# A fused LoRA kernel on one core: stores issued from ScalarE, loads from SyncE, matmuls that lower semaphores

## Chip, core and metric

One core of one Trainium2 chip. The metric is the device time of one execution in microseconds; lower is better. A core has five engines that run their own instruction streams (TensorE or PE, VectorE or DVE, ScalarE or ACT, GpSimd or POOL, SyncE or SP) and meet at semaphores, and 16 DMA engines that move data between HBM and the on-chip memory.

## The reference

```
x: (16, 512, 768) float32   A: (768, 16)   B: (16, 768)   scale = 0.5
lora = np.matmul(np.matmul(x, A), B)
return (x + scale * lora).astype(np.float32)
```

Every element of x is read once and every element of the result is written once: 25.2 MB in and 25.2 MB out, with two thin matrix products between them.

## The kernel before

**Tokens.** The 8192 tokens are 64 tiles of 128. They are held in six parts of 2, 6, 8, 16, 16 and 16 tiles (PARTS). In a part of S tiles a partition holds S tokens that lie next to each other in memory, so one partition's row in a transfer is S x 3072 bytes. The on-chip memory has three rooms of 16 tiles; ROOM says where a part lies. The last part is put where the first three parts were, so its two loads wait until these are stored.

**Transfers.** LOADS and STORES list seven transfers each, as (part, first tile, number): parts 0 to 4 whole, and part 5 in two halves. In this document L0 to L6 and S0 to S6 are these in order. All fourteen are issued by SP: L0 to L4 at once, then S0, S1 and S2, each when VectorE's sums for it are done (s_sum), then L5 when S0 and S1 have landed (s_out0), L6 when S2 has (s_out1), then S3 to S6. ScalarE issues the loads of A and B. They go into every eighth partition of a_rows and b_rows, which are cleared first by VectorE (L209) and GpSimd (L164).

**Work on a group.** Eight tiles are a group, and there are eight groups (0 to 7). L0 and L1 hold group 0, L2 group 1, L3 groups 2 and 3, L4 groups 4 and 5, L5 group 6, L6 group 7. For each group:
- narrowed() makes a float16 copy xh of x, four tiles on ScalarE (q = 0) and four on GpSimd (q = 1), all at L158;
- turned() transposes xh in 32 x 32 blocks on VectorE (L233, two instructions);
- projected() multiplies by A on TensorE (L261, 24 matmuls in three thirds);
- spread() scales that product and puts it on the diagonal blocks of y_bd, on ScalarE (L197, four instructions);
- raised() multiplies a pair of tiles by B on TensorE (L275, four matmuls) into one of two buffers lora;
- VectorE adds lora to x in place (L243, one instruction for a pair).

**Order.** Each engine's order is written out by hand. TensorE runs the four raised() of one group between the thirds of projected() of the next. Its first pass raises a group that doesn't exist, from a y_bd of zeros, to fill the loop. VectorE runs turned(g + 1) and then the four adds of g. ScalarE runs spread(g) and then narrowed(g + 2). Behind the last add of a group that ends a store VectorE drains and raises s_sum (L247). TensorE takes a semaphore in two steps, a wait and a separate sem_inc of -1 (take()); one semaphore s_free counts the lora buffers that VectorE has emptied.

**Start.** A is transposed (L211) and copied into w_one and w_bd (L218, L226) on VectorE; B is narrowed to b_half (L189), multiplied by a picking matrix (L285) and copied to b_mm (L191) on ScalarE.

Of the kernel before, what the change touches and what calls it, by code (L numbers as in the profile page):

```python
# [22 lines left out]
APART = 8  # L23
# [3 lines left out]
def kernel(  # L27
# [11 lines left out]
    Q = 32  # L39
# [39 lines left out]
    def sem(name):  # L79
        sems.append(nc.alloc_semaphore(name))  # L80
        return sems[-1]
# [9 lines left out]
    def memory(t2, i, s, n):  # L91
        S = PARTS[i]
        return t2[ds(parts[i], S * P), :].rearrange("(p s) d -> p s d", s=S)[:, ds(s, n), :]

    def held(i, s, n):
        r, s0 = ROOM[i]
        return rooms[r][:, ds(s0 + s, n), :]
# [8 lines left out]

    s_a, s_b = sem("s_a"), sem("s_b")
    s_brows, s_pick, s_bh, s_bp = sem("s_brows"), sem("s_pick"), sem("s_bh"), sem("s_bp")
    s_ready, s_zero, s_w, s_bm = sem("s_ready"), sem("s_zero"), sem("s_w"), sem("s_bm")
    s_nact, s_npool = sem("s_nact"), sem("s_npool")  # L110
    s_turned, s_y, s_spread = sem("s_turned"), sem("s_y"), sem("s_spread")
    s_lora, s_free, s_sum = sem("s_lora"), sem("s_free"), sem("s_sum")
    s_out0, s_out1, s_out = sem("s_out0"), sem("s_out1"), sem("s_out")

    MMS = 2 * NC
# [5 lines left out]
    def groups_for(i, s, n):  # L121
        return where.index((i, s + n - 1)) // GROUP + 1
# [8 lines left out]
    @block.sync  # L131
    def _(e):
        def load(ld):
            e.dma_start(out=held(*ld), in_=memory(x2, *ld)).then_inc(s_load[ld], 16)

        def store(st, done):
            e.wait_ge(s_sum, STORED.index(groups_for(*st)) + 1)
            e.dma_start(out=memory(out2, *st), in_=held(*st)).then_inc(done, 16)

        load(LOADS[0])  # L140
        for ld in LOADS[1:5]:
            load(ld)
        for st, done in zip(STORES, (s_out0, s_out0, s_out1)):
            store(st, done)
        e.wait_ge(s_out0, 32)
        load(LOADS[5])
        e.wait_ge(s_out1, 16)
        load(LOADS[6])
        for st in STORES[3:]:
            store(st, s_out)  # L150

    def narrowed(e, copy, done, g, q):
        t = g * GROUP + q * SUB
        for s in dict.fromkeys(load_sem(t + k) for k in range(SUB)):
            e.wait_ge(s, 16)
        if g >= 2:
            e.wait_ge(s_y, g - 1)
        copy(  # L158
            out=xh[g % 2][:, ds(q * SUB, SUB), :], in_=held(*where[t], SUB)
        ).then_inc(done, 1)  # L160

    @block.gpsimd
    def _(e):
        e.memset(b_rows, 0.0).then_inc(s_brows, 1)  # L164
        e.memset(pick, 0.0).then_inc(s_pick, 1)
        e.memset(w_bd.rearrange("p c k m -> p (c k m)").bitcast(fp32), 0.0)  # L166
        for t in y_bd:
            e.memset(t.rearrange("p s m -> p (s m)").bitcast(fp32), 0.0)  # L168
        e.wait_ge(s_pick, 1)
        e.affine_select(  # L170
            out=pick, in_=pick, compare_op=mybir.AluOpType.not_equal, fill=1.0, base=0,
            pattern=[[0, NQ], [-APART, Q]], channel_multiplier=1,
        ).then_inc(s_zero, 1)
        for g in range(NG):
            narrowed(e, e.tensor_copy, s_npool, g, 1)

    @block.scalar
    def _(e):
        e.wait_ge(s_brows, 1)
        e.dma_start(  # L180
            out=b_rows[0 : R * APART : APART, :], in_=B
        ).then_inc(s_b, 16)
        e.wait_ge(s_ready, 1)
        e.dma_start(
            out=a_rows[0 : NC * APART : APART, :],
            in_=A.rearrange("(c e) r -> c (e r)", e=64),
        ).then_inc(s_a, 16)
        e.wait_ge(s_b, 16)
        e.copy(out=b_half, in_=b_rows).then_inc(s_bh, 1)  # L189
        e.wait_ge(s_bp, 1)  # L190
        e.copy(out=b_mm, in_=lora[0][:, 0, :]).then_inc(s_bm, 1)  # L191

        def spread(g):
            e.wait_ge(s_y, g + 1)
            for b in range(NQ):
                q = ds(b * Q, Q)
                last = e.mul(out=y_bd[g % 2][q, :, q], in_=y_ps[g % 2][q, :, :], mul=sc)  # L197
            last.then_inc(s_spread, 1)

        narrowed(e, e.copy, s_nact, 0, 0)  # L200
        narrowed(e, e.copy, s_nact, 1, 0)
        for g in range(NG):
            spread(g)
            if g + 2 < NG:
                narrowed(e, e.copy, s_nact, g + 2, 0)

    @block.vector
    def _(e):
        e.memset(a_rows, 0.0).then_inc(s_ready, 1)  # L209
        e.wait_ge(s_a, 16)  # L210
        e.transpose(  # L211
            out=a_t[0 : NC * APART].rearrange("i k r c -> i (k r) c"),
            in_=a_rows[0 : NC * APART].rearrange("c (i k r) -> c (k r) i", k=2, r=R),
        ).then_inc(s_ready, 1)
        e.wait_ge(s_ready, 2)
        EACH = Q // APART
        for b in range(NC // EACH):
            last = e.tensor_copy(  # L218
                out=w_one[:, ds(b * EACH, EACH), :, :],
                in_=a_t[ds(b * Q, Q)].rearrange("i k r (c n) -> i c k r n", n=APART)[..., 0],  # L220
            )
        last.then_inc(s_ready, 1)
        e.wait_ge(s_ready, 3)
        e.wait_ge(s_zero, 1)
        for b in range(NQ):
            last = e.tensor_copy(out=w_bd[ds(b * Q, Q), :, :, ds(b * Q, R)], in_=w_one)  # L226
        last.then_inc(s_w, 1)

        def turned(g):
            for q, s in ((0, s_nact), (1, s_npool)):  # L230
                e.wait_ge(s, g + 1)
                v = xh[g % 2][:, ds(q * SUB, SUB), :].bitcast(fp32)
                last = e.transpose(out=v, in_=v)  # L233
            last.then_inc(s_turned, 1)

        turned(0)
        for g in range(NG):
            if g + 1 < NG:
                turned(g + 1)
            for p in range(PAIRS):  # L240
                xs = held(*where[g * GROUP + 2 * p], 2)
                e.wait_ge(s_lora, (g + 1) * PAIRS + p + 1)
                e.tensor_tensor(  # L243
                    out=xs, in0=xs, in1=lora[p % 2], op=mybir.AluOpType.add
                ).then_inc(s_free, 1)
            if g + 1 in STORED:
                e.drain().then_inc(s_sum, 1)  # L247

    @block.tensor
    def _(e):  # L250
        def take(s):
            e.wait_ge(s, 1)
            e.sem_inc(s, -1)  # L253

        def projected(h, steps):
            if steps[0] == 0:
                take(s_turned)
            xv = xh[h].rearrange("p s (c j k) -> p s c j k", c=NC, k=2)
            for m in steps:
                c, k = divmod(m, 2)  # L260
                last = e.matmul(  # L261
                    y_ps[h], w_bd[:, c, k, :], xv[:, :, c, :, k],
                    start=(m == 0), stop=(m == MMS - 1),
                )
            if steps[-1] == MMS - 1:
                last.then_inc(s_y, 1)

        def raised(h, p):
            if p == 0:
                take(s_spread)  # L270
            take(s_free)
            t = lora[p % 2]
            for k in range(2):
                for n0, w in ((0, 512), (512, 256)) if k == 0 else ((0, 256), (256, 512)):
                    last = e.matmul(  # L275
                        t[:, k, ds(n0, w)], y_bd[h][:, 2 * p + k, :], b_mm[:, ds(n0, w)],
                        start=True, stop=True,
                    )
            last.then_inc(s_lora, 1)


        e.wait_ge(s_bh, 1)
        e.wait_ge(s_zero, 1)
        for n0, w in ((0, 512), (512, 256)):
            last = e.matmul(  # L285
                lora[0][:, 0, ds(n0, w)], pick.rearrange("p b r -> p (b r)"),
                b_half[:, ds(n0, w)], start=True, stop=True,
            )
        last.then_inc(s_bp, 1)
        e.sem_inc(s_spread, 1)  # L290
        e.sem_inc(s_free, 2 + PAIRS)
        e.wait_ge(s_w, 1)
        e.wait_ge(s_bm, 1)
        with e.Fori(0, NG // 2):
            for h in range(2):
                raised(1 - h, 0)
                raised(1 - h, 1)
                projected(h, range(0, THIRD))
                raised(1 - h, 2)
                projected(h, range(THIRD, 2 * THIRD))  # L300
                raised(1 - h, 3)
                projected(h, range(2 * THIRD, MMS))
        for p in range(PAIRS):
            raised(1, p)
# [43 lines left out]
```

## Time and profile before

| | us |
|---|---|
| median of 3 runs | 124.85 (124.49 to 125.08) |
| profiled execution, its own time | 124.84 |
| its span in the profile | 122.9 |
| VectorE busy | 87.0 (71%) |
| TensorE matmuls busy | 53.9 (44%) |
| ScalarE busy | 36.9 (30%) |
| GpSimd busy | 25.6 (21%) |
| DMA, mean over the span | 410 GB/s |

Span and busy times are of one execution, and so are the lines of the profile in this document; the difference of 1.94 us between the span and the execution's own time lies outside the span. A page cuts the span into 40 slices, with a digit for the busy share in tenths. A group line ends in its busy time, the mean of one instruction, the idle time before the group's instructions and what ended it. In the timeline a line is start, duration, engine, line and operation, with the idle time before it in brackets. In the waits a line is who waited for whom, the total in us, how often, and the longest. A DMA packet in the trace's records is one partition's row, or the 4 bytes that raise a semaphore at the end.

### The profile page before, as it was taken

The page shows a single profiled execution, that of the slowest core. Times are in us where ns is not written, and L with a number is a line of the kernel's source. Part 1 is how long each engine was busy: PE and PEld are TensorE (multiplying, and loading weights), DVE is VectorE, ACT ScalarE, POOL GpSimd, SP SyncE. Part 2 cuts the span into 40 slices and gives each one's busy share as a digit, 9 for nine tenths or more (in the row PEclk, how much of TensorE's full clock was granted, in tenths as well). Part 3 has the DMA queues.
Part 4 walks back from the last instruction along what each step waited for, and adds up shares of the span by engine and source line. Part 5 has one row for each costly group of instructions (what it writes and reads, how often), then busy time and mean ns, then how long its engine had stood idle before and what let it go on. Part 6 is the DMA issues. An engine that isn't in the chain of part 4 may idle for free. (4 is left out here: it accounts for less than half of the span.)

```text
span 122.9 us, 967 instructions
## 1 busy us (share of the span) xinstructions
PE 53.9 (44%) x338; PEld 31.8 (26%) x338; DVE 87.0 (71%) x57; ACT 36.9 (30%) x43; POOL 25.6 (21%) x18
## 2 busy tenths in 40 slices
PE   0002068768306994493483477449438353000000
PEld 0000034445103562262242254236225221000000
DVE  2006993959729989999999999999999789300000
ACT  0416608220199106708504082640400400000000
POOL 7402608000196001708000080440000000000000
PEclk9999999999995599999999999999999999555555
DMA  3999999799799795999999999999899799799990
GB/s 98 429 415 450 416 528 432 336 512 480 304 496 496 320 464 228 490 418 432 456 392 464 432 400 480 400 496 448 352 480 496 336 464 466 325 456 400 456 440 40
DMA packets 2074, 50.46 MB, mean 410 GB/s; under 512 B 252, under 2 KB 252, under 8 KB 536
## 3 DMA queue, kind: packets, MB, share of 16 engines
q1 hardware_dynamic: 2016, 50.33, 96.5%
q10 hardware_dynamic: 56, 0.10, 0.2%
q8 instruction: 1, 0.02, 0.0%
q14 instruction: 1, 0.01, 0.0%
HBM read 25.26 MB, written 25.17 MB: 410 GB/s over the span
## 5 line engine op out<-in xcount | busy, mean ns | idle before, releaser
L243 DVE TENSOR_TENSOR x_sb<-x_sb,lora_ps 128x1536 f32<-128x1536 f32 x32 | 53.8, 1740 | 3.5 <-PE lora_ps L275 3.5
L275 PE MATMUL lora_ps<-b_mm,y_bd 128*128 128x512 f16 (+1 forms) x144 | 30.9, 351 | 30.8 <-PEq L253 30.8
L158 POOL CAST xh<-x_sb 128x3072 f16<-128x3072 f32 x8 | 21.9, 2746 | 55.0 <-DMA x_sb<-in_x_dram 50.5
L233 DVE STREAM_TRANSPOSE xh<-xh 128x1536 f32<-128x1536 f32 x16 | 27.5, 1755 | 5.4 <-ACT xh L158 5.0
L261 PE MATMUL ps_yt<-xh,w_bd 128*128 128x256 f16 x192 | 26.1, 277 | 9.0 <-PEq L253 9.0
L158 ACT CAST xh<-x_sb 128x3072 f16<-128x3072 f32 x8 | 22.0, 2752 | 18.2 <-DMA x_sb<-in_x_dram 18.2
L275 PEld LDWEIGHTS lora_ps<-b_mm,y_bd 128*128 128x128 f16 x144 | 13.2, 102 | 44.6 <-issue 38.9
L261 PEld LDWEIGHTS ps_yt<-xh,w_bd 128*128 128x128 f16 x192 | 18.4, 98 | 16.9 <-issue 12.0
L197 ACT ACTIVATE y_bd<-ps_yt 32x256 f16<-32x256 f32 x32 | 12.0, 374 | 34.3 <-PE ps_yt L261 34.0
L211 DVE STREAM_TRANSPOSE a_t<-a_rows 96x1024 f32<-96x1024 f32 x1 | 1.9, 1926 | 8.3 <-DMA a_rows<-in_A_dram 8.3
L285 PE MATMUL lora_ps<-b_half,pick 128*128 128x512 f16 (+1 forms) x2 | 0.8, 514 | 9.6 <-ACT b_half L189 9.6
L285 PEld LDWEIGHTS lora_ps<-b_half,pick 128*128 128x128 f16 x2 | 0.1, 110 | 9.6 <-ACT b_half L189 9.6
L218 DVE CAST w_one<-a_t 32x128 f16<-32x128 f32 x3 | 2.5, 836 | 0.1
L189 ACT ACT_TABLE_LOAD x1 | 1.3, 1283 | 3.7 <-issue 3.7
L189 ACT CAST b_half<-b_rows 128x768 f16<-128x768 f32 x1 | 0.8, 832 | 3.7 <-DMA b_rows<-in_B_dram 3.7
L209 DVE MEMSET a_rows<- 128x1024 f32 x1 | 0.9, 912 | 1.2 <-SPq L127 1.2
L166 POOL MEMSET w_bd<- 128x1536 f32 x1 | 1.4, 1382 | 0.0
L191 ACT CAST b_mm<-lora_ps 128x768 f16<-128x768 f32 x1 | 0.8, 798 | 0.9 <-PE lora_ps L285 0.9
L226 DVE COPY w_bd<-w_one 32x384 f16<-32x384 f16 x4 | 1.0, 251 | 0.1
L168 POOL MEMSET y_bd<- 128x512 f32 x2 | 1.0, 524 | 0.0
L164 POOL MEMSET b_rows<- 128x768 f32 x1 | 0.7, 737 | 0.5 <-SPq L127 0.5
L170 POOL TENSOR_SCALAR_AFFINE_SELECT pick<-pick 128x128 f16<-128x128 f16 x1 | 0.3, 309 | 0.0
(5 smaller groups left out, 0.6 us busy)
## 6 DMA issues: line engine op xcount, KB each, us to landing
x_sb<-in_x_dram SPq DMA_DIRECT2D x2, 6144.0 KB, 38.1
out_dram<-x_sb SPq DMA_DIRECT2D x2, 6144.0 KB, 22.9
x_sb<-in_x_dram SPq DMA_DIRECT2D x3, 3072.0 KB, 15.1
out_dram<-x_sb SPq DMA_DIRECT2D x3, 3072.0 KB, 16.4
x_sb<-in_x_dram SPq DMA_DIRECT2D x1, 2304.0 KB, 10.1
out_dram<-x_sb SPq DMA_DIRECT2D x1, 2304.0 KB, 22.3
x_sb<-in_x_dram SPq DMA_DIRECT2D x1, 768.0 KB, 4.5
out_dram<-x_sb SPq DMA_DIRECT2D x1, 768.0 KB, 17.2
```

The costliest lines, as they stand in the source:

```text
L158: copy(out=xh[g % 2][:, ds(q * SUB, SUB), :], in_=held(*where[t], SUB)).then_inc(done, 1)
L166: e.memset(w_bd.rearrange("p c k m -> p (c k m)").bitcast(fp32), 0.0)
L168: e.memset(t.rearrange("p s m -> p (s m)").bitcast(fp32), 0.0)
L189: e.copy(out=b_half, in_=b_rows).then_inc(s_bh, 1)
L197: last = e.mul(out=y_bd[g % 2][q, :, q], in_=y_ps[g % 2][q, :, :], mul=sc)
L211: e.transpose(out=a_t[0 : NC * APART].rearrange("i k r c -> i (k r) c"), in_=a_rows[0 : NC * APART].rearrange("c (i k r) -> c (k r) i", k= ...
L218: last = e.tensor_copy(out=w_one[:, ds(b * EACH, EACH), :, :], in_=a_t[ds(b * Q, Q)].rearrange("i k r (c n) -> i c k r n", n=APART)[..., 0],)
L226: last = e.tensor_copy(out=w_bd[ds(b * Q, Q), :, :, ds(b * Q, R)], in_=w_one)
L233: last = e.transpose(out=v, in_=v)
L243: e.tensor_tensor(out=xs, in0=xs, in1=lora[p % 2], op=mybir.AluOpType.add).then_inc(s_free, 1)
L261: last = e.matmul(y_ps[h], w_bd[:, c, k, :], xv[:, :, c, :, k], start=(m == 0), stop=(m == MMS - 1),)
L275: last = e.matmul(t[:, k, ds(n0, w)], y_bd[h][:, 2 * p + k, :], b_mm[:, ds(n0, w)], start=True, stop=True,)
```

## The change

Five things are changed together.
- Stores are issued by ScalarE: stored(g) stands behind spread(g) and narrowed(g + 2) and issues those stores whose last group is g - 1. SP issues only loads.
- A and B are issued by SP behind L1 and before L2. Both areas are cleared by GpSimd, a_rows first.
- TensorE's matmuls lower the semaphores themselves (then_inc with -1); s_free becomes four semaphores, one for each pair of a group. GpSimd sets the first values that TensorE set, and VectorE waits for the four raised() of the first pass before turned(1).
- On ScalarE narrowed(0) comes before the copy of b_mm, and narrowed() there no longer waits for s_y.
- The last s_sum is raised by the last add itself, without a drain.

```diff
-        def store(st, done):
-            e.wait_ge(s_sum, STORED.index(groups_for(*st)) + 1)
-            e.dma_start(out=memory(out2, *st), in_=held(*st)).then_inc(done, 16)
-
         load(LOADS[0])
-        for ld in LOADS[1:5]:
+        load(LOADS[1])
+        e.wait_ge(s_ready, 1)
+        e.dma_start(
+            out=a_rows[0 : NC * APART : APART, :], in_=A.rearrange("(c e) r -> c (e r)", e=64)
+        ).then_inc(s_a, 16)
+        e.wait_ge(s_brows, 1)
+        e.dma_start(out=b_rows[0 : R * APART : APART, :], in_=B).then_inc(s_b, 16)
+        for ld in LOADS[2:5]:
             load(ld)
-        for st, done in zip(STORES, (s_out0, s_out0, s_out1)):
-            store(st, done)
         e.wait_ge(s_out0, 32)
         load(LOADS[5])
         e.wait_ge(s_out1, 16)
         load(LOADS[6])
-        for st in STORES[3:]:
-            store(st, s_out)
...
-        if g >= 2:
+        if q and g >= 2:
             e.wait_ge(s_y, g - 1)
...
+        e.memset(a_rows[0 : NC * APART], 0.0).then_inc(s_ready, 1)
         e.memset(b_rows, 0.0).then_inc(s_brows, 1)
+
+        e.sem_inc(s_spread, 1)
+        for s in s_free[2:]:
+            e.sem_inc(s, 1)
...
+        def stored(groups):
+            for st in STORES:
+                if groups_for(*st) == groups:
+                    done = s_out0 if groups == 1 else s_out1 if groups == 2 else s_out
+                    e.wait_ge(s_sum, STORED.index(groups) + 1)
+                    e.dma_start(out=memory(out2, *st), in_=held(*st)).then_inc(done, 16)
+
         for g in range(NG):
             spread(g)
             if g + 2 < NG:
                 narrowed(e, e.copy, s_nact, g + 2, 0)
 
+            stored(g)
+        stored(NG)
...
         turned(0)
+        for p in range(PAIRS):
+            e.wait_ge(s_lora, p + 1)
+            e.sem_inc(s_free[p], 1)
...
-                ).then_inc(s_free, 1)
-            if g + 1 in STORED:
+                )
+                if g + 1 < NG or p + 2 < PAIRS:
+                    ins.then_inc(s_free[p], 1)
+                elif p + 1 == PAIRS:
+                    ins.then_inc(s_sum, 1)
+            if g + 1 in STORED[:-1]:
                 e.drain().then_inc(s_sum, 1)
...
-            if steps[-1] == MMS - 1:
+            if steps[0] == 0:
+                last.then_inc(s_turned, -1)
+            elif steps[-1] == MMS - 1:
                 last.then_inc(s_y, 1)
...
-                take(s_spread)
-            take(s_free)
+                e.wait_ge(s_spread, 1)
+            free = s_free[(p + 2) % PAIRS]
+            e.wait_ge(free, 1)
...
+            if p == 0:
+                mms[0].then_inc(s_spread, -1)
+            mms[1].then_inc(free, -1)
+            mms[-1].then_inc(s_lora, 1)
```

More of the change, by code (lines that the diff above doesn't have):

```diff
@@ L108 @@
     s_brows, s_pick, s_bh, s_bp = sem("s_brows"), sem("s_pick"), sem("s_bh"), sem("s_bp")
-    s_ready, s_zero, s_w, s_bm = sem("s_ready"), sem("s_zero"), sem("s_w"), sem("s_bm")
+    s_ready, s_zero, s_bm = sem("s_ready"), sem("s_zero"), sem("s_bm")
     s_nact, s_npool = sem("s_nact"), sem("s_npool")
     s_turned, s_y, s_spread = sem("s_turned"), sem("s_y"), sem("s_spread")
-    s_lora, s_free, s_sum = sem("s_lora"), sem("s_free"), sem("s_sum")
+    s_lora, s_sum = sem("s_lora"), sem("s_sum")
+    s_free = [sem(f"s_free{p}") for p in range(PAIRS)]
     s_out0, s_out1, s_out = sem("s_out0"), sem("s_out1"), sem("s_out")
@@ L178, in _ @@
     def _(e):
[L179 to L187, printed above, removed]
+        e.wait_ge(s_zero, 1)
         e.wait_ge(s_b, 16)
         e.copy(out=b_half, in_=b_rows).then_inc(s_bh, 1)
-        e.wait_ge(s_bp, 1)
-        e.copy(out=b_mm, in_=lora[0][:, 0, :]).then_inc(s_bm, 1)
         def spread(g):
@@ L200, in _ @@
         narrowed(e, e.copy, s_nact, 0, 0)
+        e.wait_ge(s_bp, 1)
+        e.copy(out=b_mm, in_=lora[0][:, 0, :]).then_inc(s_bm, 1)
         narrowed(e, e.copy, s_nact, 1, 0)
+        def stored(groups):
[4 more added lines that the diff above has]
+                    e.dma_start(out=memory(out2, *st), in_=held(*st)).then_inc(done, 16)
         for g in range(NG):
@@ L205, in _ @@
                 narrowed(e, e.copy, s_nact, g + 2, 0)
+            stored(g)
+        stored(NG)
     @block.vector
     def _(e):
-        e.memset(a_rows, 0.0).then_inc(s_ready, 1)
         e.wait_ge(s_a, 16)
@@ L225, in _ @@
         for b in range(NQ):
-            last = e.tensor_copy(out=w_bd[ds(b * Q, Q), :, :, ds(b * Q, R)], in_=w_one)
-        last.then_inc(s_w, 1)
+            e.tensor_copy(out=w_bd[ds(b * Q, Q), :, :, ds(b * Q, R)], in_=w_one)
         def turned(g):
@@ L242, in _ @@
                 e.wait_ge(s_lora, (g + 1) * PAIRS + p + 1)
-                e.tensor_tensor(
+                ins = e.tensor_tensor(
                     out=xs, in0=xs, in1=lora[p % 2], op=mybir.AluOpType.add
-                ).then_inc(s_free, 1)
-            if g + 1 in STORED:
+                )
[4 more added lines that the diff above has]
+            if g + 1 in STORED[:-1]:
                 e.drain().then_inc(s_sum, 1)
@@ L250, in _ @@
     def _(e):
-        def take(s):
-            e.wait_ge(s, 1)
-            e.sem_inc(s, -1)
         def projected(h, steps):
             if steps[0] == 0:
-                take(s_turned)
+                e.wait_ge(s_turned, 1)
             xv = xh[h].rearrange("p s (c j k) -> p s c j k", c=NC, k=2)
@@ L269, in raised @@
             if p == 0:
-                take(s_spread)
-            take(s_free)
+                e.wait_ge(s_spread, 1)
+            free = s_free[(p + 2) % PAIRS]
+            e.wait_ge(free, 1)
             t = lora[p % 2]
+            mms = []
             for k in range(2):
                 for n0, w in ((0, 512), (512, 256)) if k == 0 else ((0, 256), (256, 512)):
-                    last = e.matmul(
+                    mms.append(e.matmul(
                         t[:, k, ds(n0, w)], y_bd[h][:, 2 * p + k, :], b_mm[:, ds(n0, w)],
                         start=True, stop=True,
-                    )
-            last.then_inc(s_lora, 1)
+                    ))
+            if p == 0:
+                mms[0].then_inc(s_spread, -1)
+            mms[1].then_inc(free, -1)
+            mms[-1].then_inc(s_lora, 1)
         e.wait_ge(s_bh, 1)
-        e.wait_ge(s_zero, 1)
         for n0, w in ((0, 512), (512, 256)):
@@ L289, in _ @@
         last.then_inc(s_bp, 1)
-        e.sem_inc(s_spread, 1)
-        e.sem_inc(s_free, 2 + PAIRS)
-        e.wait_ge(s_w, 1)
         e.wait_ge(s_bm, 1)
```

## The prediction

> **What bounds the kernel now.** I read the page's table of slices first, then its DMA queues, the chain that ended last, the waits of the SP queue, the DMA issues, and last the trace's packet records.
>
> ```profile
> DVE  2006993959729989999999999999999789300000
> DMA  3999999799799795999999999999899799799990
> ```
>
> One digit is 3.07 us. VectorE is full from about 37 us to 98 us and then stops; the DMA row stays high to the end, 16 us longer.
>
> ```profile
> q1 hardware_dynamic: 2016, 50.33, 96.5%
> q10 hardware_dynamic: 56, 0.10, 0.2%
> ```
>
> Packets, MB, share of 16 engines' span: 96.7% of 122.9 is 118.8 us of work for each DMA engine. Nearly all of it is on q1, SyncE's queue; q10 is ScalarE's and holds only A and B. In the packet records the first packet starts at 1.96 us and the last ends at 121.68, so 119.7 us are open and 119.0 are used (the packets' own times, summed and divided by 16). The queue has no hole. This is the bound.
>
> ```profile
> 98.83 5.08 DVE x_sb L243 x3
> 103.92 1.66 DVEq L247
> ```
>
> The chain of waits ends at 105.58, with the last add; the remaining 17 us are stores that wait for the DMA engines. The sixth store is issued at 97.68 and its first packet starts at 105.59; the last is issued at 105.66 and starts at 113.04. So VectorE may be some 7 us later and the end doesn't move.
>
> ```profile
> SPq L138 <- DVEq L247: 83.2, 6, 29.3
> SPq L134 <- DMA out_dram<-x_sb: 15.6, 2, 8.6
> out_dram<-x_sb SPq DMA_DIRECT2D x1, 768.0 KB, 17.2
> out_dram<-x_sb SPq DMA_DIRECT2D x1, 2304.0 KB, 22.3
> ```
>
> SP's waits cost nothing, since packets are always queued ahead. I number loads L0 to L6 and stores S0 to S6 in program order. S0 is issued at 33.26 and lands at 50.50, 17.2 us for 0.23 us of packets a row: it lies behind L4 in the one queue (its first packet is at 47.34). That queue serves one packet, a partition's row, after another, 8 rows per engine and transfer: 0.234 us for 6144 B, 0.686 for 18432, 0.912 for 24576, 1.815 for 49152, loads and stores alike.
>
> **The change, part by part.** The time is the profiled execution's 124.84 us (span 122.9 and 1.94 around it); the median of the runs is 124.85.
>
> *Bytes.* The same 14 transfers of x and two small ones: 119.0 us per engine stay. Only holes in the engines' work, or rows that get longer, can move the end.
>
> *Two queues.* How two queues share an engine is seen at the start: B's rows (3072 B, q10, 0.121 us) go between two whole rows of L1, B's completion packet one more L1 row later, A likewise. So loads and stores will alternate row by row when both are there.
>
> *Stores move past ScalarE's work.* ScalarE issues in order, so each store now waits for what stands before it.
>
> ```profile
> 33.30 2.75 ACT L158 CAST xh<-x_sb 128x3072 f16<-128x3072 f32 x1 [8.01 <-DMA x_sb<-in_x_dram]
> 36.07 1.53 ACT L197 ACTIVATE y_bd<-ps_yt 32x256 f16<-32x256 f32 x4
> 37.63 2.75 ACT L158 CAST xh<-x_sb 128x3072 f16<-128x3072 f32 x1
> 48.61 2.75 ACT L158 CAST xh<-x_sb 128x3072 f16<-128x3072 f32 x1 [1.04 <-DMA x_sb<-in_x_dram]
> 70.63 2.75 ACT L158 CAST xh<-x_sb 128x3072 f16<-128x3072 f32 x1 [3.33 <-DMA x_sb<-in_x_dram]
> ```
>
> S0 and S1 come behind group 3's narrowing: 37.63 + 2.75 = 40.4 (before 33.26; the sum they need is there at 33.2). L4 then still has three rows or so per engine; up to four S0 rows go between, 4 x 0.234 = 0.9 us at most for L4 (48.58 to 49.5). S0 and S1 still finish near 55.6, as the bytes ahead are the same. S2 comes behind narrowed(4), which waits for L4: 48.6 + 2.75 = 51.4, to 52.3 (before 47.10). S3 comes behind narrowed(6), which waits for L5: 70.63 + 2.75 = 73.4 (before 67.29). S4 comes behind spread(6), 87.5 (before 87.47). S5 and S6 at 97.7 and 105.7, as before.
>
> *From issue to first packet.* Here the trace has two rows far apart: L0 on an idle SP queue, 0.94 to 1.96, 1.0 us; B on ScalarE's queue, 1.71 to 6.06 (first engine), 4.35 us. The first is another queue, the second the queue in question but among five loads being issued. I take 4.35, the same queue's own, and keep 1.0 as the other end. With 4.35: S0's rows start at 44.75, L4 is hardly moved, S2's rows start at 51.4 + 4.35 = 55.75. S1's rows end on the engines between 54.66 and 55.60, 55.2 in the mean, and L5, issued at 56.01 when S1 has landed, gives packets from 57.0 at the earliest. A hole of 0.5 us. L5 and S2 then alternate, 16 rows of 0.912, to about 70.4. L6 waits for S2 to land. S2's last row is one or two rows before the end, and landing (0.4 us in the records) and issue (1.0) eat 1.4 us, where L5's last rows give 0.9 to 1.8: taken as nothing, 0 to 0.5. L6 then runs alone for 8 x 0.912 = 7.3 us, to about 77.7; S3's rows come at 73.4 + 4.35 = 77.8, with L5 landing up to 0.4 later than now. A hole of 0.3. S4 is there at 91.9 and S3 ends near 92.5: none. Sum +0.8 us. With 1.0 for the issue: S2's rows at 52.4, S3's at 74.4, no hole, 0; with 5.5 the same steps give 3 us.
>
> *Rows that alternate.* About 26 alternations per engine (S0 with L4, S2 with L5, S3 with L6). Low end: the rows of L1 around B's, 0.686, unchanged, 0. High end: those around A's, 0.84 for 0.686, +0.15 each, 26 x 0.15 = 3.9 us. Below 0 I exclude: a row runs at 49152 B / 1.815 us = 27.1 GB/s in both directions, and the packets under way are never more than the 16 engines by more than the records' few nanoseconds. I take 0, since from 61.3 to 63.4, where S2's last and L5's first 24576 B rows lie side by side and follow each other, all but one have 0.91 to 0.92.
>
> *A and B behind L1.* They are issued once POOL has cleared their rows (0.94 + 0.9 = 1.9 and 2.6) and lie behind L1, so they land at about 11.0 and 11.2 (A now at 10.39, B at 8.66). L2's issue moves behind two waits to 3.1, but its first packet isn't due before 10.1. b_half 11.2, narrowed(0) 12.0, b_mm 15.6, transposes of group 0 at 16.6 instead of 16.00. VectorE's new wait for the four first raised() has turned(1) behind it: 3.4 us after turned(0)'s end, 23.5 instead of 21.54; TensorE's projected(1) waits for that. The first adds move from 26.44 to 27.0. The cover: VectorE idles 2.90 us before 36.08, for L3, landing at 33.27 unmoved. Without it 0.6 us of VectorE's 7 us of slack, so 0.
>
> *The rest.* TensorE loses its separate semaphore steps and VectorE one drain (under 0.1 us). VectorE is full (3.44 + 6.71 us a group) and has 7 us of slack. L6 lands near 78 to 84 (now 78.50), narrowed(7) ends by 86.5, before turned(7) at 87.54. ScalarE's seven issues, 0.3 to 1.3 us each, lie in its 70% idle time. All 0.
>
> **Sum:** 124.84 + 0.8 = 125.6 us. The forecast: slower, by the holes that ScalarE's order leaves in a queue that had none.
>
> **Rivals.**
> *No hole* (not slower). Issue takes 1.0 to 3 us on ScalarE's queue too; S2 is there before S1 ends (52.4 to 54.4 against 55.2) and S3 before L6 ends. For: SP's own row, and B's 4.35 us fell among the loads' issues. Against: it is the only row of that queue. It decides at 55.2 - 51.4 = 3.8 us from issue to first packet. 124.8 to 125.1.
>
> *Alternating rows cost.* Every row beside the other queue's is longer, as near A. At 5% of 28 us shared, +1.4 us, 126.2; at 10%, with a hole, 127.5. Against: the 0.912 rows at 61 to 63 us.
>
> *Faster.* With inputs and outputs apart, stores land early, loads are issued early, and engines overlap two rows. What the records leave to win: the slow first rows (0.7 us) and one stall in all engines at 45 us, where L4's rows took 2.3 to 3.0 us, 0.8 us. 124.0 if the stall is the one queue's doing. Against: no hole, and every other row at 27.1 GB/s. The Trainium skill, "Perfetto Trace Analysis", DMA Optimizations, advises one issuing engine for inputs and another for outputs, "to allow more dynamic spread". By that rule this rival would hold. The skill's "DMA: Bandwidth & Descriptors", Issuing engines are not separate DMA queues, says that DMAs from all engines run on the same 16 DMA engines and only sequencer time is saved. The trace agrees with this one: B's packets go between L1's, and 119.0 of 119.7 us are taken.
>
> **How the numbers follow.** A measurement of this kernel can tell about 0.5%, 0.62 us, from no change (its runs lie within 0.6 us). Holes 0.40, of which 0.30 over 0.62 us (0.8 is near that bound); no hole 0.35, all within; costly alternation 0.18, all over; faster 0.07. Slower 0.30 + 0.18 = 0.48, same 0.10 + 0.35 = 0.45, faster 0.07. The range goes from 124.3 (no hole, half of the stall gone) to 127.3 (alternation near 10%); the forecast's own is 125.0 to 126.2.
>
> **What would show it.** In the profile after: q10 with 25 MB; S2's and S3's first packets after the last of S1 and L6, as dips in the DMA row at slices 18 and 25 (from 0); rows unchanged; L6 landing at 78 to 84; VectorE's last add still near 105.6 and its stores still queued behind S4. Wrong if the row times grow (alternation), if the packets leave no gap (no hole), or if VectorE's last add comes later than about 112 and the last store starts at once.

## The result and the profile after

The changed kernel takes 125.34 us in the median of 22 executions (124.78 to 126.59), the kernel before 124.81 in 22 beside them (124.43 to 126.44). The ratio is 1.0047, 95% interval 1.0027 to 1.0068: about 0.5 us slower. The ratios here and below leave out executions that took over 1.5% more than the fastest of their kernel, which are called slow. The profiled execution is one of the shorter ones, 124.93 us with a span of 123.0.

The slices of the page after, a digit for 3.07 us:

```profile
DVE  0004984299939999979999997999999979400000
DMA  3999999699899793999999999999799999899990
```

VectorE again stops at slice 34, and the DMA row again stays high to the end. No dip lies at slices 18 and 25, where the prediction put them. A digit counts a packet where it starts, so it can fall to 7 or 3 beside a high neighbour without anything being idle. The packet records decide: from 3 us to 119 us the 16 engines together stand idle for less than 0.1 us in the mean, in the changed kernel as before.

The DMA queues (packets, MB, share of 16 engines' span):

```profile
q1 hardware_dynamic: 1064, 25.26, 49.0%
q10 hardware_dynamic: 1008, 25.17, 47.5%
```

The loads are on q1 and the stores on q10, 96.5% in all, where it was 96.7% with nearly everything on one queue.

The waits of the SP queue (who waited for whom: us in total, times, longest):

```profile
SPq L136 <- DMA out_dram<-x_sb: 61.5, 2, 51.0
```

Once the first five loads, A and B are issued, SP only waits for landed stores before L5 and L6. L6 is issued at 66.88, when S2 has landed, instead of 63.36. In the chain of waits (start, duration, what) it is S2's way from issue to landing and then L6's:

```profile
49.88 16.98 DMA out_dram<-x_sb
66.88 18.23 DMA x_sb<-in_x_dram
```

Before, SP issued L5 at 56.01 and was through with L6 7.69 us later:

```profile
56.01 7.69 SPq L134 DMA_DIRECT2D x_sb<-in_x_dram  x2
```

ScalarE's timeline, its DMA issues (ACTq) among its work:

```profile
35.95 0.37 ACT L193 ACTIVATE y_bd<-ps_yt 32x256 f16<-32x256 f32 x1
35.96 0.38 ACTq L205 DMA_DIRECT2D out_dram<-x_sb  x1
...
49.88 2.75 ACT L159 CAST xh<-x_sb 128x3072 f16<-128x3072 f32 x1 [3.44 <-DMA x_sb<-in_x_dram]
49.88 0.34 ACTq L205 DMA_DIRECT2D out_dram<-x_sb  x1
...
70.53 2.75 ACT L159 CAST xh<-x_sb 128x3072 f16<-128x3072 f32 x1 [3.43 <-DMA x_sb<-in_x_dram]
70.54 0.34 ACTq L205 DMA_DIRECT2D out_dram<-x_sb  x1
```

In the program S0 stands behind narrowed(3), S2 behind narrowed(4) and S3 behind narrowed(6). They are issued when that work is ready to start, not when it ends: S0 at 35.96, while spread(1) has only begun, S2 and S3 in the moment in which the narrowing ahead of them starts. ScalarE's queue runs ahead of its arithmetic; what holds a store back is the wait of the instruction ahead, not that instruction's duration. The Trainium skill, "Advanced Engine Details and Errata", Sequencer and Instruction Queues, says that arithmetic is pushed into a queue of the engine and the sequencer reads on; the trace agrees, with five instructions ahead of S0 not yet done at 35.96.

The start and the end on VectorE:

```profile
23.74 3.44 DVE L239 STREAM_TRANSPOSE xh<-xh 128x1536 f32<-128x1536 f32 x2 [4.03 <-PE lora_ps L290]
27.11 6.71 DVE L252 TENSOR_TENSOR x_sb<-x_sb,lora_ps 128x1536 f32<-128x1536 f32 x4
35.96 3.44 DVE L239 STREAM_TRANSPOSE xh<-xh 128x1536 f32<-128x1536 f32 x2 [2.14 <-ACT xh L159]
```

The first adds are 0.7 us later than before (26.44), and L3 hides it: turned(2) begins at 35.96, before it was 36.08.

The last pieces of the chain of waits, and two of the DMA issues (KB each, us from issue to landing):

```profile
99.20 5.08 DVE x_sb L252 x3
104.28 1.66 DVEq L319
```

```profile
out_dram<-x_sb ACTq DMA_DIRECT2D x1, 2304.0 KB, 19.7
out_dram<-x_sb ACTq DMA_DIRECT2D x1, 768.0 KB, 14.6
```

VectorE ends 0.4 us later than before, at 105.94. The last store is issued at 105.98 and its first packet starts at 112.94, so 7 us of slack are left there. S0 (768 KB) still takes 14.6 us to land: its eight rows per engine take turns with L4's long ones.

The places where the prediction put its holes: S2's first packet follows S1's last row (54.69), L6's first (69.23) follows L5's last rows, which end between 69.23 and 70.19 on the 16 engines, S3's first comes at 73.92, while L6 still has rows. Nothing is idle, yet the median is longer. That is what the experiments are about.

### The profile page after: what moved, and what is told of

Read it like the earlier page. It is cut to its first block, busy times and chain, and to the rows that moved or that the text cites. A ratio compares the mean times of both kernels' runs of the same rounds, so it can differ in the third digit from the quotient of the medians.

```text
span 123.0 us, 920 instructions
## 1 busy us (share of the span) xinstructions
PE 58.3 (47%) x338; PEld 33.8 (27%) x338; DVE 85.4 (69%) x56; ACT 36.8 (30%) x43; POOL 26.5 (22%) x19
## 4 chain that ended last, share of the span: by engine, by line
DMA 65%; PE 6%; ACT 5%; DVE 4%; SPq 2%; DVEq 1%; POOL 1%; issue 1%; ACTq 0%; POOLq 0%
DMA x_sb<-in_x_dram 52%; DMA out_dram<-x_sb 14%; DVE x_sb L252 4%; PE lora_ps L290 4%; PE ps_yt L272 2%; ACT y_bd L193 2%; ACT xh L159 2%; DVEq L319 1%; SPq L136 1%; POOL a_rows L165 1%; SPq L141 1%; SPq L145 0%; ACTq L205 0%; POOLq L356 0%; SPq L129 0%
## 5 line engine op out<-in xcount | busy, mean ns | idle before, releaser
L290 PE MATMUL lora_ps<-b_mm,y_bd 128*128 128x512 f16 (+1 forms) x144 | 33.8, 376 | 26.0 <-ACT y_bd L193 11.7
L272 PE MATMUL ps_yt<-xh,w_bd 128*128 128x256 f16 x192 | 28.5, 294 | 6.1 <-DVE xh L239 6.1
L290 PEld LDWEIGHTS lora_ps<-b_mm,y_bd 128*128 128x128 f16 x144 | 13.9, 108 | 40.7 <-issue 27.2
L272 PEld LDWEIGHTS ps_yt<-xh,w_bd 128*128 128x128 f16 x192 | 19.7, 105 | 15.2 <-DVE xh L239 8.1
L225 DVE CAST w_one<-a_t 32x128 f16<-32x128 f32 x3 | 1.8, 603 | 0.1
L165 POOL MEMSET a_rows<- 96x1024 f32 x1 | 0.9, 948 | 0.5 <-SPq L129 0.5
## 6 DMA issues: line engine op xcount, KB each, us to landing
out_dram<-x_sb ACTq DMA_DIRECT2D x1, 768.0 KB, 14.6
```

The lines of the kernel that those rows point to most:

```text
L165: e.memset(a_rows[0 : NC * APART], 0.0).then_inc(s_ready, 1)
L225: last = e.tensor_copy(out=w_one[:, ds(b * EACH, EACH), :, :], in_=a_t[ds(b * Q, Q)].rearrange("i k r (c n) -> i c k r n", n=APART)[..., 0],)
L272: last = e.matmul(y_ps[h], w_bd[:, c, k, :], xv[:, :, c, :, k], start=(m == 0), stop=(m == MMS - 1),)
L290: mms.append(e.matmul(t[:, k, ds(n0, w)], y_bd[h][:, 2 * p + k, :], b_mm[:, ds(n0, w)], start=True, stop=True,))
```

## The experiments

Each kernel was timed beside the kernel before on the same chip. The theories are numbered as in the expectations.

**e1: the stores alone.** The kernel before; SP's store() goes, and ScalarE gets the changed kernel's stored().

```diff
-        for st, done in zip(STORES, (s_out0, s_out0, s_out1)):
-            store(st, done)
...
+            stored(g)
+        stored(NG)
```

> The kernel before with one part of the change: ScalarE issues all stores behind spread(g) and narrowed(g + 2), SP issues loads alone; A, B and all semaphores as before. Theory 1 (a hole: L6 waits for S2 to land, S2 now shares the engines row by row with L5, so L6's first packet is at times later than L5's last): this part alone gives the whole loss, 1.003 to 1.007 of before, 125.1 to 125.7 us. Rival 2 (rows that alternate between the queues take longer): the same 1.003 to 1.007, but the rows of L5 and S2 would be longer than 0.912 us in the mean by 1% or more. Rival 3 (the start with A and B behind L1, or the new semaphores): 0.999 to 1.001, 124.7 to 124.9 us.

Measured: 125.11 us in the median of 12, ratio 1.0015, 0.9988 to 1.0041. The interval holds nothing and nearly the whole loss, so alone it decides nothing. L6 is issued at 67.02, as late as in the changed kernel; any account of the loss by this lateness has to allow for a ratio as small as this.

**e2: all but the stores.** The changed kernel with its stores issued by SP, in the order of the kernel before.

```diff
+        for st, done in zip(STORES, (s_out0, s_out0, s_out1)):
+            store(st, done)
         e.wait_ge(s_out0, 32)
...
-            stored(g)
-        stored(NG)
```

> The changed kernel with its stores back on SP, in the place and order of the kernel before; A and B behind L1 and the matmuls lowering semaphores stay. Theory 1 (hole at L6) and rival 2 (longer rows) both give the time of before, 0.999 to 1.001, 124.7 to 124.9 us. Rival 3 (start or semaphores) gives 1.003 to 1.007, 125.1 to 125.7 us.

Measured: 124.91 us, ratio 0.9990, 0.9963 to 1.0016. A and B behind L1, the new semaphores, VectorE's new wait and the missing drain together cost nothing that these runs can tell. Rival 3 is out: the loss comes with the stores' move. Since the stores alone (e1) gave 1.0015 and the whole change 1.0047, it isn't shown that the move alone gives all of it.

**e3: S2 ahead of L5 on SP.** Meant to free L6 of its wait.

```diff
             load(ld)
+        e.wait_ge(s_sum, 2)
+        e.dma_start(out=memory(out2, *STORES[2]), in_=held(*STORES[2])).then_inc(s_out1, 16)
         e.wait_ge(s_out0, 32)
```

> The changed kernel with only S2 issued by SP, ahead of L5 in the same queue; all other stores stay on ScalarE. S2 then lands near 63.3 us and L6 is queued before L5 ends. S0 still alternates with L4, and S3 with L6. Theory 1 (hole at L6): the loss is gone, 0.999 to 1.002, 124.7 to 125.0 us. Rival 2 (alternating rows): more than half of the alternations are taken away, about half of the loss stays, 1.002 to 1.003. Rival 3 (start or semaphores): all of it stays, 1.003 to 1.007.

Measured: 128.86 us, ratio 1.0328, 1.0295 to 1.0360; no theory expected it. The waits of its SP queue, and its engines in two windows (length, busy us of PE, PEld, DVE, ACT and POOL, the clock, DMA share, GB/s):

```profile
SPq L149 <- DVEq L262: 41.5, 1, 41.5
SPq L136 <- DMA out_dram<-x_sb: 16.4, 1, 16.4
```

```profile
56.00:62.00 6.00, 2.84 (x18) 1.60 (x19) 6.00 (x5) 3.40 (x3) 1.97 (x1) 1.00 0.98 419
62.00:64.00 2.00, 2.00 (x16) 1.28 (x15) 2.00 (x2) 0.00 (x0) 0.00 (x0) 1.00 0.00 0
```

S2, issued at 46.51 into SP's now empty queue, didn't wait its turn behind S1: from 50.34, when S0 was done, it alternated with S1 row by row, and S1's last row ended at 61.98 instead of 55.64. L5 waits for S1, and by 62.89 both queues were empty: until L5's first packets at 64.23 an engine stands idle for 2.27 us in the mean. The edit moved the wait to another place. It does show what a real hole looks like (a share of 0.00) and that it is not given back. Rows of L5 and L6 behind it are longer too, by 0.7 and 1.3 us per engine.

**e4: S2 later.** The changed kernel with S2 behind spread(3).

```diff
             spread(g)
+            if g == 3:
+                stored(2)
             if g + 2 < NG:
                 narrowed(e, e.copy, s_nact, g + 2, 0)

-            stored(g)
+            if g != 2:
+                stored(g)
```

> The changed kernel with S2 issued one step later on ScalarE, behind spread(3) at about 56 us instead of 49.9. S1's rows end at 54.8 to 55.6 and nothing else is queued. Theory 1: a hole of 1 to 3 us at 55 to 58, and a second one of 1 to 2 us at about 71, since S2 then lands with L5; each us of hole is a us at the end, 127.0 to 129.0 us in all. Rival 2 or 3: holes at these places are covered elsewhere, 125.0 to 126.0 us.

Measured: 127.73, 127.74 and 127.97 us, ratio 1.0235, 1.0195 to 1.0276; a fourth execution took 133.68 and is not in the ratio, and it is the one with the profile. The time is as theory 1 says. The holes are so in part: in this profile an engine stands idle for 2.2 us in the mean between 54 and 58, as expected, but for 0.15 us and not 1 to 2 at 72 to 74, and for 2.7 us at 96 to 100, where nobody expected it. It doesn't tell whether the changed kernel has a hole.

**a1, a2, a3: the changed kernel again.**

> The changed kernel itself, again, on the chip of e5. Theory 1, 2 and 3 all expect 1.003 to 1.007 of before. Its profile, if it falls on one of the longer executions (over 125.3 us), shows under theory 1 idle DMA engines of 0.4 to 1.8 us at about 69 to 72 us; under rival 2 rows over 0.92 us (24576 B) or 1.83 us (49152 B) in the mean; under rival 3 a wider spread of the last rows' ends.

> A further profiled execution of the changed kernel, for one of the longer ones. Theory 1: if over 125.3 us, idle engines at 69 to 72 us. Rival 2: longer rows. Rival 3: last rows' ends further apart. If under 125.0: none of these.

> A further profiled execution of the changed kernel, for one of the longer ones. Theory 1: if over 125.3 us, idle engines at 69 to 72 us. Rival 2: longer rows. Rival 3: last rows' ends further apart. If under 125.0: none of these.

Measured: a1 125.37 us, ratio 1.0045, 1.0013 to 1.0076. Its profiled execution is a longer one, 125.58; a2's is 125.01 and a3's 124.88. In none of them are the engines idle: a1 has 0.002 us between 68 and 76. Theory 1 falls, as a1 was one of the longer executions that it was to explain. In a1, 16 of L6's 128 rows take over 1.0 us, up to 1.83 instead of 0.91, most of them at 72 to 75; that is 0.39 us per engine. They aren't spread evenly: the last packet ends at 122.16, against 121.69 in the first profile, and the 16 engines end 2.0 us apart, against 1.5, and the rows of S2, L5 and S3 are as usual. So rows are longer, as rival 2 has it, but the worst three start at 72.2 to 72.6, where L6 runs alone (S3's first packet is at 74.30), and ends lie further apart, as rival 3 has it. From this came theory 4: L6 is issued too late, 2.3 us before its first packet is due.

**e5: L6 without a wait.** The changed kernel with room of its own for L6, so that it is issued right behind L5. For lack of memory a_rows, a_t and b_rows lie in the same place, used only at the start. S2 then raises s_out as the later stores do.

```diff
+    own = sb("x_sb3", [P, 8, D], fp32)
...
+        if i == 5 and s >= 8:
+            return own[:, ds(s - 8, n), :]
...
         load(LOADS[5])
-        e.wait_ge(s_out1, 16)
         load(LOADS[6])
```

> The changed kernel with L6 in a room of its own (its start overlaid on a_rows, a_t and b_rows, which are dead by then), so that L6 no longer waits for S2 to land and is issued right behind L5 at about 56 us. Theory 1 (in part of its executions the changed kernel has a hole where L6, late behind S2's landing, comes after L5's last row): the loss is gone, 0.998 to 1.001 of before, 124.6 to 125.0 us, and no executions over 125.3 beyond those that the kernel before has too. Rival 2 (what alternation itself does to rows or to the evenness of the 16 engines): L6 still alternates with S3, S2 with L5, S0 with L4, so 1.003 to 1.006 stays. Rival 3 (the length of the tail: one engine later than the others at the end): 1.002 to 1.006 stays, and the last rows' ends lie over 1.4 us apart.

> The kernel of e5 again, beside e6 on the same chip. Theory 4: 0.999 to 1.002 of before and 0.3 to 0.5% below e6. Rival 5: equal to e6. If e5's first result was chance: 1.003 to 1.006, equal to the changed kernel.

SP's queue in the first of its two profiles:

```profile
3.47 53.66 SPq L140 DMA_DIRECT2D x_sb<-in_x_dram  x5
```

L6's issue begins at 56.33 and is over at 57.13.

Measured: 124.81 us, ratio 1.0013, 0.9983 to 1.0042, where a1 on the same chip had 125.37; again 124.77 us, ratio 1.0006, 0.9981 to 1.0030. The loss is gone, though S0 with L4, S2 with L5 and S3 with L6 alternate as in the changed kernel and S3 is issued at the same time (70.47). Alternation at those places costs nothing that can be measured: rival 2 is out. The engines' last rows end 1.6 us apart, the sign that rival 3 named, but its loss isn't there.

**e6: the room, with the wait.**

```diff
         load(LOADS[5])
+        e.wait_ge(s_out1, 16)
         load(LOADS[6])
```

> The kernel of e5 (L6 in a room of its own) in which L6 waits for S2 to land all the same, as in the changed kernel; only the wait differs from e5, only the place in memory from the changed kernel. Theory 4, formed from a1 (no hole; L6, issued at 66.9 only 2.3 us before its first packet, has rows lengthened by up to 0.9 us at 72 to 75, on some engines more than on others): the loss is there again, 1.003 to 1.006 of before, 125.1 to 125.5 us. Rival 5 (the place in memory made e5 shorter): as e5, 0.999 to 1.002.

Measured: 125.40 us, ratio 1.0038, 1.0009 to 1.0067. On the same chip e5 had 124.77. The room didn't help; the wait costs.

**e8: the room, with another wait.**

```diff
         load(LOADS[5])
+        e.wait_ge(s_sum, 3)
         load(LOADS[6])
```

> The kernel of e5 (L6 in a room of its own) with L6 held back by VectorE's sums of group 3 instead of S2's landing: issued at about 67.2 us, 2 us before its first packet, whatever the stores do. Theory 4 (the lateness of L6's issue is what costs): as e6, 1.002 to 1.006 of before, 125.1 to 125.5 us. Rival 7 (what costs in e6 and the changed kernel is that L6 hangs on S2's slowest engine, not when it is issued): as e5, 0.999 to 1.002, 124.7 to 125.0 us.

What SP waited for in e6, and then in e8:

```profile
SPq L140 <- DMA out_dram<-x_sb: 61.5, 2, 51.0
```

```profile
SPq L140 <- DMA out_dram<-x_sb: 51.0, 1, 51.0
SPq L140 <- DVEq L264: 10.4, 1, 10.4
```

Measured: 125.51 us, ratio 1.0059, 1.0034 to 1.0084. L6 was issued at 66.88, in e6 at 66.82, and what it waited for was VectorE, not S2. A wait ahead of L6 isn't enough: e2 has one, with L6 issued at 63.40, and no loss. So it is the time of L6's issue that costs, and S2 matters only because it sets that time.

The same in single executions, all sets together: under 124.75 us are 44 of 107 of the kernel before, none of 36 of the changed kernel, 10 of 24 of e5, 1 of 24 of e6 and e8, and of e1, with L6 as late, 1 of 12. The mark of 124.75 was chosen afterwards; of the kernel before it holds between 6 of 22 and 14 of 23, by set.

**e7: S3 earlier.** The changed kernel with S3 ahead of narrowed(6).

```diff
             spread(g)
+            if g == 4:
+                stored(g)
             if g + 2 < NG:
                 narrowed(e, e.copy, s_nact, g + 2, 0)

-            stored(g)
+            if g != 4:
+                stored(g)
```

> The changed kernel with S3 issued ahead of narrowed(6) on ScalarE, at about 67.3 us instead of 70.5; L6 waits as in the changed kernel. S3's packets then start near 70.5 and alternate with nearly all of L6's, which lands near 88 instead of 85; VectorE is some 3 to 5 us later in group 7, within its 7 us of slack. Rival 6 (it is the start of S3's packets beside L6 running alone that lengthens L6's rows): the long rows move to 69 to 72 us, the loss stays or shrinks, 1.000 to 1.005. Theory 4 (L6 is issued too late): the long rows stay with L6's first half, the loss stays, 1.003 to 1.006. If VectorE's slack doesn't hold: over 1.008.

Measured: 131.04 us in the median of six (128.87 to 131.19; no interval) against 124.80, the last of the outcomes named. Its waits of ScalarE and of VectorE, its timeline of ScalarE, and two windows with the columns as in e3:

```profile
ACT xh L159 <- DMA x_sb<-in_x_dram: 33.0, 5, 16.9
```

```profile
DVE xh L242 <- ACT xh L159: 13.4, 3, 10.4
```

```profile
67.07 0.34 ACTq L205 DMA_DIRECT2D out_dram<-x_sb  x1
...
95.26 2.75 ACT L159 CAST xh<-x_sb 128x3072 f16<-128x3072 f32 x1 [16.89 <-DMA x_sb<-in_x_dram]
95.28 0.34 ACTq L205 DMA_DIRECT2D out_dram<-x_sb  x1
```

```profile
84.00:92.00 8.00, 2.12 (x17) 1.23 (x14) 3.68 (x3) 0.00 (x0) 0.00 (x0) 0.79 0.86 342
92.00:96.00 4.00, 0.00 (x0) 0.00 (x0) 0.00 (x0) 0.74 (x1) 0.71 (x1) 0.50 0.26 111
```

A turn is a row, and a row of S3 has 49152 B where one of L6 has 24576. So L6 gets a third of the engines while S3 is there, and lands at about 95 instead of 85. VectorE waits 10.4 us for it and ScalarE 16.9, where S4 stands behind narrowed(7): S4 is issued at 95.28 instead of 88.10, and the engines run dry. It doesn't tell theory 4 from rival 6: the three rows of L6 over 1.0 us start at 69.4 to 70.2, where both expect them. Rival 6 as an account of the loss falls with e5, where S3 starts beside L6 in the same way (its first packet at 73.81) and the loss is gone. It shows how near the edge the changed kernel's order stands: S3 3.5 us earlier costs 6 us.

No version was found that beats the kernel before: e5, the best, is level with it.

## Why the prediction was right or wrong

The size and the sign were right (0.8 us forecast, 0.5 measured); the mechanism was not, so that the size came near is luck. The 0.8 us were two holes of 0.5 and 0.3 us, and none of the four profiles of the changed kernel has either.

- *The bound*: right. The DMA engines are never idle and VectorE's end moved only from 105.58 to 105.94.
- *A and B, the start, the rest at 0*: right. The first adds were put at 27.0 and came at 27.11, turned(1) at 23.5 and 23.74; e2 has the ratio 0.9990 for all of it.
- *Stores past ScalarE's work*: wrong. The step counted the narrowing's 2.75 us before each issue. S0 was issued at 35.96 and not at 40.4, S2 at 49.88 and not at 51.4, S3 at 70.54 and not at 73.4.
- *From issue to first packet*: taken as 4.35 us, measured 3.57 for S0, 3.32 for L5 beside S2 and 3.38 for S3. Between the two ends, and nearer to the one taken. With the issues at their true times both holes close: S2's packets are ready before S1's last row ends, and S3's come 8 us before L6's last. In the prediction's own sum either of the two steps put right closes both holes: 51.4 + 3.57 = 55.0 or 49.88 + 4.35 = 54.2 against 55.2 for S2, and 73.4 + 3.38 = 76.8 or 70.54 + 4.35 = 74.9 against 77.7 for S3.
- *L6, "0 to 0.5, taken as nothing"*: the loss lies at this place, 0.5 us, in a form that wasn't thought of. L6 comes without a gap, but is issued late, and e5, e6 and e8 show that the late issue is what costs. S2's landing is later than was reckoned as well: its completion packets, too, wait for a row of L5, so that S2's last row ends at 65.64 and it lands at 66.86.
- *Alternating rows at 0*: right in the changed kernel (e5). In e7, where 49152 B rows alternate long with L6's, they took 2.00 us in the mean instead of 1.82.
- *The rivals.* No hole was the true state of the engines, with a loss all the same: 125.34 us, where that rival put 124.8 to 125.1. Faster wasn't seen: e1 has no gain from separate queues. That is against the advice of the Trainium skill, "Perfetto Trace Analysis", DMA Optimizations, in this kernel, which has no idle DMA time to win.

Open: how lateness becomes time. Longer rows of L6 are no mark of it. a1 has them in one longer execution, but the profiles of e6 and e8 fell on shorter ones (124.89 and 124.93, with 0.18 and 0.06 us of longer rows per engine), and the kernel before has 0.18 at the same load too. In e3 L6 was issued 8.4 us before its first packet and has the most, 33 rows over 1.0 us. In the kernel before, e1, e2, e3 and a1 most of these rows start in the last 3 us before S3's first packet, wherever that lies (74.30 in a1, 76.56 before, 78.07 in e3), which is what rival 6 says of the rows; yet e5, with S3 starting at the same place, has 0 and 1 of them. What makes a row longer wasn't found.

One rival wasn't tried. The time ends with the last of the 16 engines. In the first profile of the changed kernel, in a2, in e5's first and in e8, that engine had served a 16 KB instruction fetch (q8) among S5's rows, 0.93 us and 0.4 us more for the row behind it, and it ended 0.4 to 0.6 us after all others. In e5's second profile, of 124.45 us, no such fetch came before the last packet, and the end is 121.16 instead of 121.55. So where this fetch falls can be worth about as much as the loss (0.49 us between the two executions of e5, if nothing else set them apart). Whether it falls there more often in one kernel than in another isn't known. It isn't what made a1 a longer execution: there the engines that ended last were others.

## What to carry to other kernels

When the DMA engines are full, look for what a new wait does to the time at which a transfer is issued, even where the packets then leave no gap: here 66.9 us for a packet due at 69.2 cost 0.4 to 0.6% in the changed kernel, e6 and e8, though only 0.15% in e1, where 63.4 (e2) and 56.3 (e5) cost nothing that could be told. In these records two queues share the engines row by row, so a transfer with long rows takes more than its half from one with short rows (e7); know which transfer the next stage waits for before moving one of them to a queue of its own. A DMA issue that stands behind arithmetic on ScalarE waited for the waits ahead of it and not for the arithmetic (S0, S2 and S3).

## What the runs showed that was not expected

- In every profile L4's last rows, in progress at about 46.4 us, take 2.2 to 3.1 us instead of 1.82, on all 16 engines: 0.7 to 1.0 us per engine, whatever is queued behind. So it isn't the one queue's doing, as one rival had it. Its cause wasn't tried.
- From issue to first packet it is 0.8 to 1.0 us on idle engines (L0; L5 in e3, S4 in e7) and 3.3 to 3.7 us beside a busy other queue (S0, L5 and S3 in the four profiles of the changed kernel).
- One row in each profile loses 0.35 us beside a transfer of 8 KB on q14, and one 0.4 us in most of them near the one on q8, both instruction fetches; they fall on single engines, which are themselves busy with the fetch for 0.31 and 0.93 us, and make their ends uneven.
